# Output projection of a hybrid decoder layer: the order written by hand, operands summed on TensorE, filling steps dealt anew

## The chip, the cores and the metric

The kernel runs on one core of one Trainium2 chip, in one launch. The metric is the device time of the program in microseconds (us), the median of several runs.

## The reference, cut to what matters

One decoder layer on a sequence of 1024 rows of 1024 float32 features: two groups of attention heads, one output projection for both, two normalised residual additions, a feed-forward part of width 2816 and a gated embedding.

```python
xn = rmsnorm(h, pre_mix_norm)
proj = xn @ w_in
ret_out = silu(rg) * head_groupnorm(retention(rope(rq), rope(rk), rv))   # 4 heads of 128
mla_out = mla_causal(q, k, v)                                            # 8 heads, values of 64
mix = concatenate([ret_out, mla_out]) @ w_o
h = h + rmsnorm(mix, post_mix_norm)
hn = rmsnorm(h, pre_ffn_norm)
ff = (silu(hn @ w_gate) * (hn @ w_up)) @ w_down
h = h + rmsnorm(ff, post_ffn_norm)
h = h + rmsnorm(p @ w_ple_proj, ple_norm) * sigmoid(h @ w_ple_gate + b_ple_gate)
```

## The kernel before

Rows are worked in 8 tiles of 128. A float32 product is made of three matmuls on TensorE (PE): each operand is split into a rounded high part and the rest (`split`, L79: a cast on ScalarE, ACT, and a subtraction on VectorE, DVE, or on GpSimd, POOL), and `products` (L89) adds high by high, high by rest and rest by high in a PSUM bank.

**Attention and filling (L576 to L655).** Eight heads run one after the other, each in two halves (`gg`) of two groups (`g`). The first half of the output projection, retention's 512 features by `w_o`, does not depend on these heads. It is the filling: a generator (`product_to`, L546) of 16 steps of 12 matmuls each, two for a row tile, whose results go to memory (`od`). `advance(gen, tag, n)` (L557) lets n steps run. Heads 2 to 5 take 2 steps after their first half and 1 after their second, heads 6 and 7 take 1 after the first, and L655 runs the 2 that are left after the last head.

**Output projection (L705 to L765).** For each of 8 tiles, in the order 0, 2, 4, 6, 1, 3, 5, 7, `project` splits the tile's attention features (`mt` into `mh`, `ml`), multiplies them by the second half of `w_o` (24 matmuls into a double PSUM bank `po3`; there are two such banks), adds the filling's result in `mix` (L715, DVE), takes the root of the mean square (ACT's Square at L717 writes its squares into the PSUM bank; L111 on DVE, L113 on POOL), scales (L719), adds the residual rows in `ht` (L720), stores them to `hd`, takes a second root (Square at L723, again into the bank) and scales again (L725 on DVE, L726 on ACT). `operands` (L728) turns the normalised rows into the operands of the feed-forward part, which multiplies in 7 block products instead of 8, so that it needs sums of blocks: for the first four tiles two transposed halves (B11, B21), for the last four four differences t1 to t4 on POOL (L739 to L742) and five transposed blocks T2, T1, T3, B22, T4. A block is four 128x128 transposes on PE (`to_operand`, L681, into `ptx`), a cast on ACT and a subtraction on DVE. The banks for `ptx` go round in the order t, f, t, o, where t has two.

**Feed-forward part (from L889).** `load(m)` fetches a quarter of a weight matrix, `weight_part` splits it, `weight_sums` makes four sums on POOL, `product(m, n)` is 12 matmuls (`gu`), `evict` empties a bank.

**What sets the order.** Each engine runs its queue in order. A scheduler with times of its own deals the instructions to the queues, so that code order is only a wish, until the `manual_schedule` at L948: under it the order of the code is kept. DMAs all go through SyncE's (SP's) queue.

Of the kernel before, what the change touches and what calls it, by code (L numbers as in the profile page):

```python
# [11 lines left out]
F32 = mybir.dt.float32  # L12
F32R = mybir.dt.float32r
# [49 lines left out]
def hybrid_layer(ctx: ExitStack, tc: tile.TileContext, a: dict, out: bass.AP):  # L63
# [57 lines left out]
    pad.tile([P, 8], F32, name="pad")  # L121
    pack = const.tile([P, sum(PACK.values())], F32, name="pack")
    mhalf = const.tile([P, 32], F32, name="mhalf")
    pool.memset(mhalf, -0.5)

    views, off = {}, 0
# [446 lines left out]
    pm = scoped(st2, "pm", 2)  # L573
    vb = None

    for h in range(NH):  # L576
        kh_, kl_, qh, ql = heads(h) if h else first
        if h == 2:
# [13 lines left out]
        for gg in range(2):  # L592
            cs = slice(gg * 512, (gg + 1) * 512)
            po = ps1("po", "of"[gg] if h >= 3 else "o")
            for g in (2 * gg, 2 * gg + 1):
                pb = []
                sc = ps2("sc") if g < 2 else None
                for i in (2 * g, 2 * g + 1):
                    n = (i + 1) * P
                    c1 = slice(i * P, (i + 1) * P)  # L600
                    if g >= 2:
                        sc = ps2("sc")
                    o = (i % 2) * 512 if g < 2 else 0
                    nc_ = 1 if n <= 512 else 2
                    w = max(n // nc_, 256)
                    for c in range(nc_):
                        products(sc[:, o + c * 512 : o + c * 512 + w],
                                 [(qh[:, c1], ql[:, c1], kh_[:, c * w : (c + 1) * w], kl_[:, c * w : (c + 1) * w])])
                    w = n // nc_
                    sv = sc[:, o : o + nc_ * 512].rearrange("p (c n) -> p c n", c=nc_)[:, :, :w]  # L610
                    nm = small.tile([P, 1], F32, name="nm")
                    dve.tensor_tensor_reduce(  # L612
                        out=sv, in0=sv, in1=cmask[:, S - n :].rearrange("p (c n) -> p c n", c=nc_),
                        scale=-1.0, scalar=3.0e38, op0=ALU.add, op1=ALU.min, accum_out=nm)
                    pr_ = pm.tile([P, S], F32, name="pr", bufs=5)
                    rs = small.tile([P, 1], F32, name="rs")
                    act.activation(pr_[:, :n].rearrange("p (c n) -> p c n", c=nc_), sv, AF.Exp, bias=nm, scale=-1.0,  # L617
                                   accum_out=rs)
                    ri = small.tile([P, 1], F32, name="ri")
                    dve.reciprocal(out=ri, in_=rs)  # L620
                    pool.tensor_tensor(out=pr_[:, :n], in0=pr_[:, :n], in1=ri.broadcast_to([P, n]), op=ALU.mult)  # L621
                    pb.append(pr_)
                last = 2 * g + 1
                for jj in range(g + 1):
                    blk = [(2 * jj, 0), (2 * jj, 1), (2 * jj + 1, 0), (2 * jj + 1, 1)]
                    if jj == g:
                        blk = [blk[0], blk[1], blk[3]]
                    pt = ps1("ptp")
                    for m, (kk, qq) in enumerate(blk):
                        pe.transpose(pt[:, m * P : (m + 1) * P], pb[qq][:, kk * P : (kk + 1) * P], ident)  # L630
                    nn = len(blk) * P
                    th = pm.tile([P, 512], F32R, name="th", bufs=4)[:, :nn]
                    tl = pm.tile([P, 512], F32R, name="tl", bufs=4)[:, :nn]
                    split(th, tl, pt[:, :nn])
                    off = (g % 2) * 256
                    for kk in (2 * jj, 2 * jj + 1):
                        if kk < last:
                            src, dst = slice((kk % 2) * 256, (kk % 2) * 256 + 256), slice(off, off + 256)
                        else:
                            src, dst = slice(256, 384), slice(off + 128, off + 256)  # L640
                        pe.matmul(po[:, dst], vt[:, kk, :], th[:, src], start=(kk == 0), stop=False)  # L641
                        pe.matmul(po[:, dst], vt[:, kk, :], tl[:, src], start=False, stop=(kk == last))  # L642
            if h >= 2:
                advance(gen, "fo"[gg], (2, 1)[gg] if h < 6 else 1 - gg)
            os_ = pm.tile([P, 512], F32, name="os")
            rows = slice((h % 2) * 64, (h % 2) * 64 + 64)
            act.copy(out=os_[rows], in_=po[64:])
            dve.tensor_tensor(out=os_[rows], in0=po[:64], in1=os_[rows], op=ALU.add)
            for i in range(4):
                sp.dma_start(out=mo[4 * gg + i][rows, h // 2, :], in_=os_[rows, i * P : (i + 1) * P])  # L650
        if h == 4:
            wo2 = [slot(a["w_o"][4 + k], name=f"o{4 + k}", hl=(bh[1][:, k, :], bl[1][:, k, :])) for k in range(4)]

    act.activation(small.tile([P, 1], F32, name="warm", bufs=1), rs, AF.Silu)
    advance(gen, "f", 2 * NT)  # L655
    st2.close()
    st3.close()
# [23 lines left out]
    def to_operand(i, j, src, tags="tfto"):  # L681
# [1 line left out]
        pt = ps1("ptx", tags[nblk % len(tags)])  # L683
        nblk += 1
        for k in range(4):
            pe.transpose(pt[:, k * P : (k + 1) * P], src[:, k * P : (k + 1) * P], ident)
        js = slice(j * P, (j + 1) * P)
        split(xs[i][0][:, :, js], xs[i][1][:, :, js], pt.rearrange("p (k n) -> p k n", k=4))

# [12 lines left out]
        sp.dma_start(out=blk[n % 7], in_=od[t])  # L702
        sp.dma_start(out=blk[7 + n % 3], in_=a["x"][t * P : (t + 1) * P])

    def project(n):  # L705
        t = order[n]
        mt = mts[n]
        mh, ml = [pmo.tile([P, 4, P], F32R, name=n_) for n_ in ("mh", "ml")]
        mix, ht = blk[n % 7], blk[7 + n % 3]
        split(mh, ml, mt, sub=pool)  # L710
        pt = ps2("po3")
        for c in range(2):
            cs = slice(c * 512, (c + 1) * 512)
            products(pt[:, cs], [(mh[:, k, :], ml[:, k, :], wo2[k][0][:, cs], wo2[k][1][:, cs]) for k in range(4)])
        dve.tensor_tensor(out=mix, in0=pt, in1=mix, op=ALU.add)  # L715
        ss = small.tile([P, 1], F32, name="s3")
        act.activation(pt, mix, AF.Square, accum_out=ss)  # L717
        rsqrt(ss, ss, 1.0 / D)
        dve.scalar_tensor_tensor(out=mix, in0=mix, scalar=ss, in1=wpm, op0=ALU.mult, op1=ALU.mult)  # L719
        dve.tensor_tensor(out=ht, in0=ht, in1=mix, op=ALU.add)  # L720
        sp.dma_start(out=hd[t], in_=ht)
        ss = small.tile([P, 1], F32, name="s3")
        act.activation(pt, ht, AF.Square, accum_out=ss)  # L723
        rsqrt(ss, ss, 1.0 / D)
        dve.tensor_tensor(out=mix, in0=ht, in1=wpf, op=ALU.mult)  # L725
        act.activation(mix, mix, AF.Copy, scale=ss)  # L726

    def operands(n, part=None):  # L728
        j = n % 4
        mix = blk[n % 7]  # L730
        if n < 4:
            to_operand(B11, j, mix[:, lo_])
            to_operand(B21, j, mix[:, hi_])
        else:
            e, ht = blk[j], blk[7 + n % 3]
            t1, t2, t3, t4 = e[:, lo_], ht[:, lo_], mix[:, lo_], e[:, hi_]
            b11, b12, b21, b22 = e[:, lo_], mix[:, lo_], e[:, hi_], mix[:, hi_]
            if part != 1:
                pool.tensor_tensor(out=t1, in0=b12, in1=b11, op=ALU.subtract)  # L739
                pool.tensor_tensor(out=t2, in0=b22, in1=t1, op=ALU.subtract)  # L740
                pool.tensor_tensor(out=t3, in0=b22, in1=b12, op=ALU.subtract)
                pool.tensor_tensor(out=t4, in0=b21, in1=t2, op=ALU.subtract)  # L742
            for i, src in ((T2, t2), (T1, t1), (T3, t3), (B22, b22), (T4, t4))[slice(*((0, 5), (2, 5), (0, 2))[part or 0])]:
                to_operand(i, j, src)

    load_rows(0)
    load_rows(1)
    load_tiles(0)
    for v, name in ((wpm, "w_post"), (wpf, "w_pref")):
        sp.dma_start(out=v, in_=a[name].broadcast_to([P, D]))  # L750
    for n in range(1, 4):
        if n > 1:
            load_rows(n)
        if n < 3:
            load_tiles(n)
    for n in range(NT):
        if n == 7:
            load_tiles(7)
        project(n)
        if n % 4 < 2:  # L760
            load_rows(n + (4 if n < 4 else 2))
        if n >= 2:
            operands(n - 2)
        if n < 4:
            load_tiles(n + 3)  # L765
    st_m.close()
    st_b.close()

# [118 lines left out]
        todo[i].append((f, args))  # L887

    load(0)  # L889
    load(1)  # L890
    weight_part(0, 0)
    weight_part(1, 0)
    operands(NT - 2)
    for m, n in steps[:2]:
        product(m, n)
    operands(NT - 1, 2)
    for m, n in steps[2:4]:
        product(m, n)
    for m in range(2):
        weight_sums(m)  # L900
    for m, n in steps[:4]:
        evict(m, n)


    for q in range(NQ):
# [42 lines left out]
    with tc.manual_schedule():  # L948
        for i, (m, n) in enumerate(steps):
            if i < 4:  # L950
                continue
            for f, args in todo[i]:
                f(*args)
            if i == 6:
                operands(NT - 1, 1)
            product(m, n)
            evict(m, n)
    st_g.close()
# [209 lines left out]
```

## Time and profile before

| what | value |
| --- | --- |
| median of 3 runs | 1400.54 us (1399.19 to 1403.55) |
| the profiled execution: its own time | 1400.68 us |
| the profiled execution: span from first to last instruction | 1398.9 us |
| granted TensorE clock, mean over the span | 0.986 |
| PE busy | 1336.5 us, 96% of the span |
| DVE, ACT, POOL busy | 770.9, 541.8, 461.8 us |

The profiled execution's time is 0.14 us over the median, and lies 1.8 us over its span. A matmul's end is modelled in the profile, so that PE's busy time is a little more than PE's work: what a matmul takes of a dense row of them is the distance between two starts. The granted clock is 1.0 where the engine has its full 2.4 GHz and 0.5 where it has 1.2 GHz.

### The profile page before, as it was taken

To read this page: it belongs to the slowest core of one execution; us is meant where nothing else is said; L and a number is where in the kernel's file an instruction comes from. 1 tells how busy PE (TensorE), PEld (TensorE's weight loads), DVE (VectorE), ACT (ScalarE), POOL (GpSimd) and SP (SyncE) were. 2 spreads that over 40 slices of the span, in tenths; PEclk is the share of its full clock that TensorE was granted. 3 is DMA by queue.
4 is the path that set the end of the run, shared out by engine and by line. 5 is a ranking of instruction groups with operands and counts; after the bars stand their busy time and mean duration, and the time that the engine had idled before them with its cause. 6 is when DMAs were issued, how large, how long until landed. Compare 5 with 4: busy or idle time off the path is not lost.

```text
span 1398.9 us, 18091 instructions
## 1 busy us (share of the span) xinstructions
PE 1336.5 (96%) x6756; PEld 1134.4 (81%) x6756; DVE 770.9 (55%) x1193; ACT 541.8 (39%) x898; POOL 461.8 (33%) x341
## 2 busy tenths in 40 slices
PE   7999999999989999887999999999999999999997
PEld 6987988988778887665788888888888788888886
DVE  6445637445566676488445444444445554474645
ACT  5443321011565555355343333333334444344521
POOL 1100000000363333248577666666664100012500
PEclk9999999999999999998999999999999999999999
DMA  7127831212474641743344344433346876565422
GB/s 251 46 92 250 265 118 39 75 23 60 143 232 123 200 131 30 273 135 123 121 165 149 146 173 173 169 138 144 140 178 218 269 234 211 178 218 193 138 102 75
DMA packets 85304, 214.73 MB, mean 153 GB/s; under 512 B 8992, under 2 KB 23840, under 8 KB 79584
## 3 DMA queue, kind: packets, MB, share of 16 engines
q1 hardware_dynamic: 85216, 213.58, 45.5%
q8 instruction: 53, 0.87, 0.3%
q14 instruction: 35, 0.29, 0.1%
HBM read 144.86 MB, written 67.63 MB: 152 GB/s over the span
## 4 chain that ended last, share of the span: by engine, by line
PE 83%; DMA 4%; DVE 4%; POOL 3%; issue 3%; ACT 2%; SPq 1%; DVEq 0%; ACTq 0%; POOLq 0%
PE gu L834 29%; PE db L1011 7%; PE pqk L94 6%; PE pg L94 6%; PE da L1011 6%; PE pa L94 4%; PE fill L94 3%; PE prv L94 3%; PE sc L94 3%; PE ptp L630 2%; PE prg L94 2%; PE pge L94 2%; PE po L642 1%; PE pq L94 1%; PE po L641 1%
## 5 line engine op out<-in xcount | busy, mean ns | idle before, releaser
L834 PE MATMUL gu<-x,gh 128*128 128x512 f32 x1232 | 383.6, 393 | 6.3 <-ACT po L723 5.6
L834 PEld LDWEIGHTS gu<-x,gh 128*128 128x128 f32 x1232 | 233.2, 190 | 55.7 <-ACT po L723 5.8
L834 PE MATMUL gu<-x,gl 128*128 128x512 f32 x616 | 241.2, 392 | 0.4 <-DVE gl L82 0.4
L834 PEld LDWEIGHTS gu<-x,gl 128*128 128x128 f32 x616 | 116.7, 189 | 25.1 <-DVE gl L82 0.7
L845 ACT COPY duo<-gu 128x512 f32<-128x512 f32 x66 | 38.9, 589 | 189.3 <-PE gu L834 189.3
L621 POOL TENSOR_TENSOR pr<-pr,ri 128x128 f32<-128x128 f32 (+3 forms) x64 | 74.8, 1178 | 105.7 <-DVE ri L620 98.4
L113 POOL TENSOR_TENSOR s<-s,mhalf 128x1 f32<-128x1 f32 x32 | 23.9, 752 | 238.4 <-DVE s L111 238.3
L113 POOL TENSOR_TENSOR gf<-gf,mhalf 128x4 f32<-128x4 f32 x8 | 8.1, 1008 | 266.7 <-DVE gf L111 266.7
L82 DVE TENSOR_TENSOR gl<-strip,gh 128x1024 fp32r<-128x1024 f32 (+1 forms) x44 | 61.6, 1399 | 33.3 <-ACT gh L81 33.3
L82 DVE TENSOR_TENSOR x<-draw,x 128x1024 fp32r<-128x1024 f32 (+1 forms) x43 | 48.1, 1135 | 46.9 <-ACT x L81 46.9
L82 DVE TENSOR_TENSOR gl<-graw,gh 128x1024 fp32r<-128x1024 f32 x22 | 33.8, 1538 | 72.5 <-ACT gh L81 72.5
L81 ACT CAST x<-draw 128x1024 fp32r<-128x1024 f32 (+1 forms) x47 | 45.2, 979 | 73.0 <-PE db L1011 20.6
L82 DVE TENSOR_TENSOR gl<-duo,gh 128x1024 fp32r<-128x1024 f32 x22 | 29.5, 1343 | 67.9 <-ACT gh L81 67.9
L850 DVE TENSOR_TENSOR duo<-gu,duo 128x512 f32<-128x512 f32 x66 | 45.4, 687 | 38.0 <-PE gu L834 37.9
L82 DVE TENSOR_TENSOR tl<-ptp,th 128x512 fp32r<-128x512 f32 (+1 forms) x80 | 49.8, 633 | 24.7 <-ACT th L81 23.7
L94 PE MATMUL pg<-x,x 128*128 128x512 f32 (+1 forms) x255 | 58.9, 378 | 0.0
L81 ACT CAST th<-ptp 128x512 fp32r<-128x512 f32 (+1 forms) x80 | 42.4, 544 | 41.9 <-PE ptp L630 41.6
L855 POOL TENSOR_TENSOR duo<-duo 128x512 f32<-128x512 f32 x11 | 23.3, 2122 | 103.2 <-DVE duo L818 103.2
L617 ACT ACTIVATE pr<-sc,nm 128x128 f32<-128x128 f32 (+3 forms) x64 | 47.7, 747 | 18.7 <-DVE nm L612 11.1
L94 PEld LDWEIGHTS pg<-x,x 128*128 128x128 f32 x255 | 45.8, 188 | 8.6
L612 DVE CUSTOM_DVE_ANT_0 sc<-sc,cmask 128x128 f32<-128x128 f32 (+3 forms) x64 | 48.0, 770 | 7.7 <-PE sc L94 7.3
L94 PE MATMUL pqk<-bl,hi_r 128*128 128x512 f32 x128 | 50.7, 396 | 0.0
(368 smaller groups left out, 3418.5 us busy)
## 6 DMA issues: line engine op xcount, KB each, us to landing
draw<-ld SPq DMA_DIRECT2D x58, 256.0 KB, 3.8
graw<-in_w_gate SPq DMA_DIRECT2D x11, 1024.0 KB, 8.6
duo<-in_w_up SPq DMA_DIRECT2D x11, 1024.0 KB, 4.7
duo<-in_w_down SPq DMA_DIRECT2D x11, 1024.0 KB, 5.1
td<-duo SPq DMA_DIRECT2D x11, 1024.0 KB, 4.4
ld<-duo SPq DMA_DIRECT2D x11, 1024.0 KB, 4.4
draw<-td SPq DMA_DIRECT2D x36, 256.0 KB, 4.1
ld<-duo SPq DMA_DIRECT2D x11, 768.0 KB, 6.7
```

The source lines that it names most:

```text
L81: act.copy(out=hi, in_=src)
L82: sub.tensor_tensor(out=lo, in0=src, in1=hi.bitcast(F32), op=ALU.subtract)
L94: pe.matmul(dst, l, r, start=(m == 0), stop=(m == n - 1))
L113: pool.tensor_tensor(out=dst, in0=dst, in1=mhalf[:, :n], op=ALU.pow)
L612: dve.tensor_tensor_reduce(out=sv, in0=sv, in1=cmask[:, S - n :].rearrange("p (c n) -> p c n", c=nc_), scale=-1.0, scalar=3.0e38, op0=ALU. ...
L617: act.activation(pr_[:, :n].rearrange("p (c n) -> p c n", c=nc_), sv, AF.Exp, bias=nm, scale=-1.0, accum_out=rs)
L621: pool.tensor_tensor(out=pr_[:, :n], in0=pr_[:, :n], in1=ri.broadcast_to([P, n]), op=ALU.mult)
L630: pe.transpose(pt[:, m * P : (m + 1) * P], pb[qq][:, kk * P : (kk + 1) * P], ident)
L834: pe.matmul(dst, l[:, at, ks], r[:, k, :], start=(n in (0, 1, 3) and x == 0), stop=(x == 11), skip_group_check=True)
L845: act.copy(out=s[nm], in_=dst)
L850: dve.tensor_tensor(out=s[nm], in0=dst, in1=s[nm], op=ALU.add)
L1011: pe.matmul(banks[j], l[:, ls], r[:, rs_], start=(fresh and q == 0 and m == 0), stop=(q == NQ - 1 and m == 2), skip_group_check=True)
```

## The change

- The order of the output projection and of the start of the feed-forward part is written by hand: `manual_schedule` now encloses L756 ff. and L889 ff. A turn `turn(n)` works three tiles at once: tile n's sum, roots and scaling, tile n - 1's second root and last scaling, tile n - 2's operands, and the matmuls of tile n + 1, whose rows were split a turn earlier.
- Square writes its squares to `junk`, a corner of the operand T4 in SBUF, no longer into the PSUM bank.
- POOL makes two differences a tile (t1, t3) in place of four. T2 = b22 - t1 and T4 = b21 - b22 + t1 are summed in PSUM: each 128x128 block is multiplied by the identity or by its negative (`minus`) as an ordinary float32 matmul, 2 and 3 of them where one transpose stood.
- The 16 filling steps are dealt anew: heads 2 to 7 take 1, 3, 2, 2, 2 and 0; three stand in the last group of head 7, one ahead of each of its first three pairs of products; 3 are left after the last head.

```diff
+    FILL = (0, 1), (2, 1), (1, 1), (1, 1), (1, 1), (0, 0)
...
+                    if h == NH - 1 and g == 3 and jj < 3:
+                        advance(gen, "o", 1)
...
-                advance(gen, "fo"[gg], (2, 1)[gg] if h < 6 else 1 - gg)
+                advance(gen, "fo"[gg], FILL[h - 2][gg])
...
+    dve.tensor_scalar(out=minus, in0=ident, scalar1=-1.0, scalar2=None, op0=ALU.mult)
...
-            pe.transpose(pt[:, k * P : (k + 1) * P], src[:, k * P : (k + 1) * P], ident)
+            ks = slice(k * P, (k + 1) * P)
+            if len(src) == 1:
+                pe.transpose(pt[:, ks], src[0][:, ks], ident)
+                continue
+
+            for n, v in enumerate(src):
+                pe.matmul(pt[:, ks], v[:, ks], (ident, minus)[n % 2], start=(n == 0), stop=(n == len(src) - 1))
...
+    def squares(n, i, v):
+        ss = roots[n, i] = small.tile([P, 1], F32, name="s3")
+        act.activation(junk, v.rearrange("p (b n) -> p b n", b=8), AF.Square, accum_out=ss)
+
+    def sums(n):
+        e, mix, ht = blk[n % 4], blk[n % 7], blk[7 + n % 3]
+        pool.tensor_tensor(out=ht[:, lo_], in0=mix[:, lo_], in1=e[:, lo_], op=ALU.subtract)
+        pool.tensor_tensor(out=ht[:, hi_], in0=mix[:, hi_], in1=mix[:, lo_], op=ALU.subtract)
...
+        return [(T2, j, (b22, t1)), (T1, j, (t1,)), (T3, j, (t3,)), (B22, j, (b22,)), (T4, j, (b21, b22, t1))]
...
+    def turn(n):
+        mix, ht = blk[n % 7], blk[7 + n % 3]
+        own, last = n < NT, 1 <= n
+        ops = operand_list(n - 2) if n >= 2 else []
+        if own:
+            dve.tensor_tensor(out=mix, in0=banks_o[n], in1=mix, op=ALU.add)
+        if last:
+            rsqrt(roots[n - 1, 1], roots[n - 1, 1], 1.0 / D)
+        for o in ops[:2]:
+            to_operand(*o)
+        if own:
+            squares(n, 0, mix)
+        if last:
+            act.activation(blk[(n - 1) % 7], blk[(n - 1) % 7], AF.Copy, scale=roots[n - 1, 1])
+        if own:
+            rsqrt(roots[n, 0], roots[n, 0], 1.0 / D)
+        if n - 1 >= 4:
+            sums(n - 1)
+        for o in ops[2:]:
+            to_operand(*o)
+        if own:
+            if n + 2 < NT:
+                prepare(n + 2)
+            if n + 1 < NT:
+                out_product(n + 1)
+            dve.scalar_tensor_tensor(out=mix, in0=mix, scalar=roots[n, 0], in1=wpm, op0=ALU.mult, op1=ALU.mult)
+            dve.tensor_tensor(out=ht, in0=ht, in1=mix, op=ALU.add)
+            sp.dma_start(out=hd[order[n]], in_=ht)
+            squares(n, 1, ht)
+            dve.tensor_tensor(out=mix, in0=ht, in1=wpf, op=ALU.mult)
...
+    with tc.manual_schedule():
+        turn(NT - 1)
+        load(1)
+        weight_part(0, 0)
+        for m, n in steps[:2]:
+            product(m, n)
+        turn(NT)
+        weight_part(1, 0)
+        for m, n in steps[2:4]:
+            product(m, n)
+        for o in operand_list(NT - 1)[:2]:
+            to_operand(*o)
+        for m in range(2):
+            weight_sums(m)
+        for m, n in steps[:4]:
+            evict(m, n)
...
+            if i == 6:
+                for o in operand_list(NT - 1)[2:]:
+                    to_operand(*o)
```

What stands in DVE's queue in the middle of the output projection, before (`duo` holds `mix` and `ht`; L715 adds the projection, L719 scales, L720 adds the residual, L725 multiplies by the next norm's weights, L111 belongs to a root, L82 is an operand's rest):

```order
L111 TENSOR_SCALAR s_5940<-s_5940 128x1
L719 SCALAR_TENSOR_TENSOR duo_5741<-duo_5741,s_5940,strip 128x1024
L720 TENSOR_TENSOR duo_5742<-duo_5742,duo_5741 128x1024
L715 TENSOR_TENSOR duo_5738<-po_5973,duo_5738 128x1024
L725 TENSOR_TENSOR duo_5741<-duo_5742,strip 128x1024
L111 TENSOR_SCALAR s_5947<-s_5947 128x1
L82 TENSOR_TENSOR x_5728<-ptx,x_5728 128x4x128
L82 TENSOR_TENSOR x_5729<-ptx,x_5729 128x4x128
L111 TENSOR_SCALAR s_5999<-s_5999 128x1
```

The same place after the change (L755, L775, L776 and L779 are the former L715, L719, L720 and L725):

```order
L111 TENSOR_SCALAR s_5962<-s_5962 128x1
L775 SCALAR_TENSOR_TENSOR duo_5743<-duo_5743,s_5962,strip 128x1024
L776 TENSOR_TENSOR duo_5744<-duo_5744,duo_5743 128x1024
L779 TENSOR_TENSOR duo_5743<-duo_5744,strip 128x1024
L755 TENSOR_TENSOR duo_5740<-po_5971,duo_5740 128x1024
L111 TENSOR_SCALAR s_5999<-s_5999 128x1
L82 TENSOR_TENSOR x_5730<-ptx,x_5730 128x4x128
L82 TENSOR_TENSOR x_5731<-ptx,x_5731 128x4x128
L111 TENSOR_SCALAR s_6022<-s_6022 128x1
```

The multiplication by the weights moved from behind the next tile's sum to ahead of it.

What stands in ACT's queue where the feed-forward part begins, before (L717 and L723 are the two Squares of the last tile, `gh` the high half of the first weights, `x` those of the operands):

```order
L726 ACTIVATE duo_5740<-duo_5740,s_6122 128x1024
L81 CAST x_5734<-ptx 128x4x128
L81 CAST gh_6262<-graw 128x1024
L81 CAST x_5733<-ptx 128x4x128
L81 CAST x_5731<-ptx 128x4x128
L717 ACTIVATE po_6173,s_6199<-duo_5741 128x1024
L81 CAST x_5730<-ptx 128x4x128
L81 CAST gh_6256<-duo_5738 128x1024
L81 CAST x_5732<-ptx 128x4x128
L845 COPY duo_5739<-gu 128x512
L723 ACTIVATE po_6173,s_6206<-duo_5742 128x1024
```

The same place after the change (L733 is Square, L763 the last scaling):

```order
L733 ACTIVATE x_5736,s_6250<-duo_5743 128x8x128
L763 ACTIVATE duo_5742<-duo_5742,s_6206 128x1024
L81 CAST x_5734<-ptx 128x4x128
L81 CAST x_5735<-ptx 128x4x128
L81 CAST x_5736<-ptx 128x4x128
L733 ACTIVATE x_5736,s_6289<-duo_5744 128x8x128
L81 CAST gh_6223<-graw 128x1024
L81 CAST x_5732<-ptx 128x4x128
L81 CAST x_5733<-ptx 128x4x128
L763 ACTIVATE duo_5743<-duo_5743,s_6289 128x1024
```

The first weights' cast moved from ahead of both Squares of the last tile to behind both.

## Rows read from the trace of the kernel before

**Rows 1.** Stretches of core 0: us, busy time (instructions) of each engine, granted clock, DMA.
```profile
550.00:572.00 22.00, 17.95 (x71) 14.15 (x72) 6.19 (x11) 7.52 (x14) 2.92 (x2) 0.77 0.21 57
572.00:681.00 109.00, 85.63 (x379) 67.73 (x378) 76.81 (x82) 51.93 (x82) 63.56 (x51) 0.89 0.47 170
...
650.00:660.00 10.00, 4.42 (x20) 3.49 (x19) 8.70 (x8) 4.36 (x8) 8.77 (x6) 0.79 0.13 52
```

**Rows 2.** Timeline of PE: start, us, line, operation; two matmuls of a projection.
```profile
574.17 0.39 PE L94 MATMUL po<-bh,ml 128*128 128x512 f32 x1
574.40 0.39 PE L94 MATMUL po<-bh,mh 128*128 128x512 f32 x1
```

**Rows 3.** PE in the retention: float32 matmuls (`psc`), transposes (`pkt`), the next start.
```profile
308.02 1.05 PE L462 MATMUL psc<-qk 128*128 128x128 f32 x8
308.91 0.60 PE L469 MATMUL pkt<-pack,qk 128*128 128x128 f32 x4
309.27 0.48 PE L94 MATMUL pqk<-bh,hi_r 128*128 128x512 f32 x1
```

**Rows 4.** Instructions of the tile `psc`: count, ns min/median/max.
```profile
L462 PE MATMUL psc<-qk x64: 270/275/275, 197.1 to 348.1; 128*128 128x128 f32 x64
```

**Rows 5.** Chain that ended last: twelve operand transposes at full clock.
```profile
679.55 1.31 PE ptx L686 x12
```

**Rows 6.** What PE waited for from 540 to 720: us in total, times, longest.
```profile
PE po L94 <- ACT po L723: 9.2, 6, 3.6
PE gu L834 <- ACT po L723: 5.6, 1, 5.6
PE ptx L686 <- POOL duo L740: 2.6, 3, 1.2
PE ptx L686 <- DVE x L82: 2.1, 1, 2.1
PE ptx L686 <- POOL duo L739: 1.8, 1, 1.8
...
PE ptx L686 <- POOL duo L741: 1.1, 1, 1.1
```

**Rows 7.** Single lines from 560 to 690: count, ns min/median/max, first and last start.
```profile
L715 DVE TENSOR_TENSOR duo<-po,duo x8: 1210/1218/1225, 578.1 to 646.3; 128x1024 f32<-128x1024 f32 x8
L717 ACT ACTIVATE po<-duo x8: 1029/1034/1047, 579.3 to 647.6; 128x1024 f32<-128x1024 f32 x8
L717 ACT ACTIVATION_READ_ACCUMULATOR po<-duo x8: 186/193/202, 580.3 to 648.5; 128x1 f32 x8
L719 DVE SCALAR_TENSOR_TENSOR duo<-duo,s,strip x8: 1283/1284/2344, 581.3 to 651.3; 128x1024 f32<-128x1024 f32 x8
L720 DVE TENSOR_TENSOR duo<-duo,duo x7: 1224/2168/2277, 582.6 to 654.7; 128x1024 f32<-128x1024 f32 x7
L725 DVE TENSOR_TENSOR duo<-duo,strip x8: 1207/1430/1728, 584.9 to 657.5; 128x1024 f32<-128x1024 f32 x8
L111 DVE TENSOR_SCALAR s<-s x16: 136/141/154, 580.5 to 659.7; 128x1 f32<-128x1 f32 x16
L113 POOL TENSOR_TENSOR s<-s,mhalf x16: 541/550/560, 580.7 to 663.7; 128x1 f32<-128x1 f32 x16
```

**Rows 8.** Operand and weight splits: tiles `ptx` and `gh`.
```profile
L81 ACT CAST x<-ptx x28: 565/586/611, 594.7 to 682.0; 128x512 fp32r<-128x512 f32 x28
L82 DVE TENSOR_TENSOR x<-ptx,x x28: 673/676/692, 595.3 to 683.9; 128x512 fp32r<-128x512 f32 x28
L81 ACT CAST gh<-graw x2: 1052/1054/1056, 643.0 to 677.3; 128x1024 fp32r<-128x1024 f32 x2
```

**Rows 9.** POOL's differences of two tiles (L740) from 560 to 690.
```profile
L740 POOL TENSOR_TENSOR duo<-duo,duo x2: 2128/2129/2130, 624.4 to 634.6; 128x512 f32<-128x512 f32 x2
L740 POOL TENSOR_TENSOR duo<-duo x2: 1281/1438/1596, 644.0 to 667.8; 128x512 f32<-128x512 f32 x2
```

**Rows 10.** The DMAs of L702 that fetch a tile of `od`.
```profile
DMA to landing us min/median/max: 5.1/8.3/11.0
```

More of the change, by code (lines that the diff above doesn't have):

```diff
@@ L123, in hybrid_layer @@
     mhalf = const.tile([P, 32], F32, name="mhalf")
+    minus = const.tile([P, P], F32, name="minus")
     pool.memset(mhalf, -0.5)
@@ L703, in load_tiles, with prepare, out_product @@
         sp.dma_start(out=blk[7 + n % 3], in_=a["x"][t * P : (t + 1) * P])
[L705 to L711, printed above, removed]
+    junk = xt[6][:, :, :, 3 * P :].rearrange("p h k n -> p (h k) n")
+    split_rows, banks_o, roots = {}, {}, {}
+    def prepare(n):
+        split_rows[n] = [pmo.tile([P, 4, P], F32R, name=n_) for n_ in ("mh", "ml")]
+        split(*split_rows[n], mts[n], sub=pool)
+    def out_product(n):
+        mh, ml = split_rows[n]
+        pt = banks_o[n] = ps2("po3")
         for c in range(2):
@@ L714, in project, with operand_list @@
             products(pt[:, cs], [(mh[:, k, :], ml[:, k, :], wo2[k][0][:, cs], wo2[k][1][:, cs]) for k in range(4)])
[L715 to L728, printed above, removed]
+    def squares(n, i, v):
[5 more added lines that the diff above has]
+        pool.tensor_tensor(out=ht[:, hi_], in0=mix[:, hi_], in1=mix[:, lo_], op=ALU.subtract)
+    def operand_list(n):
         j = n % 4
@@ L731, in operands @@
         if n < 4:
[L732 to L744, printed above, removed]
+            return [(B11, j, [mix[:, lo_]]), (B21, j, [mix[:, hi_]])]
+        e, ht = blk[j], blk[7 + n % 3]
+        b21, b22, t1, t3 = e[:, hi_], mix[:, hi_], ht[:, lo_], ht[:, hi_]
+        return [(T2, j, (b22, t1)), (T1, j, (t1,)), (T3, j, (t3,)), (B22, j, (b22,)), (T4, j, (b21, b22, t1))]
[29 more added lines that the diff above has]
+            dve.tensor_tensor(out=mix, in0=ht, in1=wpf, op=ALU.mult)
     load_rows(0)
@@ L750, in hybrid_layer @@
         sp.dma_start(out=v, in_=a[name].broadcast_to([P, D]))
[L751 to L765, printed above, removed]
+    load_rows(2)
+    load_tiles(1)
+    load_rows(3)
+    load_tiles(2)
+    with tc.manual_schedule():
+        prepare(0)
+        load_rows(4)
+        prepare(1)
+        load_rows(5)
+        out_product(0)
+        for n in range(NT - 1):
+            turn(n)
+            if n < 4:
+                load_tiles(n + 3)
+            if n in (2, 3):
+                load_rows(n + 4)
+            if n == 6:
+                load_tiles(7)
     st_m.close()
@@ L889, in hybrid_layer @@
     load(0)
[L890 to L902, printed above, removed]
+    with tc.manual_schedule():
+        turn(NT - 1)
[13 more added lines that the diff above has]
+            evict(m, n)
     for q in range(NQ):
```

2 lines of the change are left out of this document (removed).

## The prediction

> **What bounds the kernel now.** I read the page's busy times first: PE is busy for 96% of the span, so that most stages are limited by PE's own work and the change can win only where PE waits. The stretches come next [rows 1]. From 550 to 572 (the last head's second half and what is left of the filling) and from 572 to 681 (the output projection, up to the last operand of the feed-forward part) the granted clock is 0.77 and 0.89, where the whole span has 0.986. These are the two places that the change touches. In the second, PE's work at full clock is 192 matmuls of the projection and 72 of the feed-forward part at 0.23 us from start to start [rows 2] and 112 operand transposes at 1.31/12 = 0.109 us [rows 5], that is 60.7 + 12.2 = 72.9 of 109.0 us. So 36 us there are waits, half clock and short gaps. The list of waits names most of them [rows 6]: the next projection and the first weights' product wait for the Square that still holds the PSUM bank (9.2 + 5.6 us), the operands for POOL's differences (2.6 + 1.8 + 1.1) and for a bank that DVE has not emptied (2.1). Together 22.4 us.
>
> **What the change removes.** Square no longer writes to the bank, so the first two waits, 14.8 us, lose their cause. T2 and T4 no longer come from POOL, whose second difference takes 1.28 to 2.13 us [rows 9]. All 22.4 us are taken off, since every queue is dealt anew, and what waits in the new order is counted below.
>
> **PE's added work.** Four tiles each have 8 + 12 ordinary float32 matmuls where 8 transposes stood: 80 matmuls for 32 transposes. The retention has both kinds side by side [rows 3]: eight instructions of `psc` fill 308.91 - 308.02 = 0.89 us, four transposes 0.36. The code asks for 32 products in `psc` and the trace has 64 [rows 4], so one product is two instructions, 0.222 us; a transpose is one, 0.09 to 0.109. The work grows by 80 x 0.222 - 32 x 0.109 = 17.8 - 3.5 = **14.3 us**. It is certain as work, and it lies on the path unless it falls into a pause; its place is between the last projections and the first weights' products, where PE is what everything waits for. The Trainium skill (TensorE: Matmul & The Clock Gate, Terms) says that transpose mode is 4x faster for FP32. By that an estimate would be 80 x 0.436 - 3.5 = 31.4 us of added work; the rows show a factor of 2, and they decide.
>
> **A turn in the middle.** The order rows of DVE show the new loop. Tile n's Square needs its sum (L715); the sum now stands behind the weights' multiplication (L725) of the tile before, and that one behind the residual sum (L720), which needs the scaling (L719), which needs the root. Per turn [rows 7]: Square 1.03 + 0.19, L111 0.14, L113 0.55, L719 1.28, L720 1.22 alone or 2.17 beside POOL's split, L725 1.43, L715 1.22, which is 7.1 to 8.0, with 0.2 for the hand-offs 7.3 to 8.2 us. PE has 24 x 0.228 + 8 x 0.109 = 6.3 us of work in such a turn. So PE pauses 1.0 to 1.9 us in each of five turns; I take 1.4, together **7.0 us** (5.0 to 9.5). Before, the sum stood ahead of the multiplication, and the same loop was shorter by 1.43.
>
> **The first tile with five operands.** T4 goes into the bank that T2 had, and T2's rest (L82, on DVE) stands behind a sum and a multiplication. **2.0 us**, the nearest row being the 2.1 us that PE waits for such a bank now [rows 6]; 0 to 4.
>
> **The start of the feed-forward part.** The order rows of ACT show that the first weights' cast now stands behind both Squares of the last tile. In DVE's queue, from that tile's sum on: sum 1.22, root 0.14, T2's rest 0.68; then PE's twelve matmuls of T4, 2.66; T4's cast and rest, 0.59 + 0.68 [rows 8]; scaling 1.28, residual sum 1.22 to 2.17, Square 1.22, the weights' cast 1.05: 10.7 to 11.7, taken as 11.2 us. PE has 20 x 0.222 + 12 x 0.109 = 5.7 us of operands meanwhile. The sum itself waits for the last tile of `od`: its fetch stands in SP's queue behind the store of the tile before, which waits for that tile's residual sum, and such a fetch lands 5.1 us after its issue at the least [rows 10]. The residual sum and the last projection's matmuls (5.5 us) run at about the same time; I take 4 us from the end of these matmuls to the landing, 0 to 8. So PE pauses 4 + 11.2 - 5.7 = **9.5 us** (5 to 14).
>
> **Behind it.** The second weights' cast stands behind five casts of operands: the cast 1.05 and its rest, less what runs beside, **2.5 us** (1 to 4). The last tile's T2 is cast behind the casts of weight sums, which wait for POOL; six of POOL's operations of 1.3 to 2.1 us [rows 9] run against 7.7 us of PE's work, **4.0 us** (0 to 8). New pauses in all: 7.0 + 2.0 + 9.5 + 2.5 + 4.0 = 25.0 us, 11 to 39.5.
>
> **The filling.** From 550 to 572 PE is busy for 17.95 of 22 us, and a granted clock of 0.77 means 10.1 us at 1.2 GHz, which cost 5.1 [rows 1]: at most 9.1 us to win. Three steps of 12 x 0.228 = 2.7 us now stand in the last group, where they cover the softmax's round through DVE, ACT and POOL and should keep the clock up. They are not new work; four steps fewer stand in heads 2 to 6 and open pauses there, 0 to 2.7 us each. I take the clock's 5.1 less 1.8, **3.3 us** won (0 to 9.1).
>
> **The clock from 572 to 681.** 0.89 of 109 us means 24 us at 1.2 GHz, at most 12.0 us lost [rows 1]. The pauses that brought it down go, others as long come: no term, -12 to +6 in the range.
>
> **The sum.** 14.3 - 22.4 + 25.0 - 3.3 = +13.6 us. Against the profiled execution's own 1400.68 us, which is 0.14 over the median, this is 1414 us, 1% slower.
>
> **The rivals.**
> 1. PE is fed. The place is the loop of a turn: if the sum finds DVE free and the loop falls to PE's 6.3 us, the turns lose nothing; with that, the last tile's sums run earlier against PE, so that the 9.5 us become 3. It decides where the new pauses are 11 us or less, as the lower bounds say. With 3 us of half clock saved: 14.3 - 22.4 + 11 - 3.3 - 3 = -3.4, 1397; with the filling's whole 9.1, 1391. For it speaks that the bank is freed 6 us earlier, against it that DVE's loop is longer by L725 in the rows themselves. Taken at 1393, faster.
> 2. A draw: the new pauses are 15 instead of 25 us, and a little clock is won: 1402.
> 3. The clock stays up. From 650 to 660, with PE busy for 4.42 us and POOL for 8.77, the granted clock is 0.79 [rows 1]. If more matmuls and shorter pauses keep it at full from 572 to 681, up to 12.0 us come back: 1414 - 9 = 1405, still slower. The Trainium skill (TensorE: Matmul & The Clock Gate, Part 4: PE-mode transpose) says that transposes do not count as busy for the gate the way matmuls do, which speaks for this rival; in the rows nothing separates the two, and the pauses of the start, 9.5 us, remain.
> 4. The plain float32 matmul with the identity costs four transposes: 14.3 becomes 31.4, 1431. The 64 instructions of `psc` speak against it.
>
> **How the numbers follow.** Chances: forecast (1407 to 1422) 0.72, PE fed 0.10, draw 0.07, clock up 0.09, four transposes 0.02. The likeliest gives **1414 us**. About 0.3%, 4.2 us, is what a measurement of this kernel can tell from no change. Faster by more, under 1396.3: 0.10. Within: the draw's 0.07. Slower, over 1404.7: the rest, 0.83. The range leaves out the fed case and the four transposes, and part of the draw: 1401 to 1422.
>
> **What would show it.** In the changed kernel's profile: `ptx` has 80 more PE instructions on the line of `matmul` in `to_operand` than products, 160 in all, at 0.11 us each from start to start; the Square is gone from the list of PE's waits; turns four to six are 7.3 to 8.2 us apart; the longest pause of PE is ahead of the first `gu` and its releaser is ACT's cast of `gh`; the clock from 550 to 565 is full. The prediction is wrong if turns are 6.5 us apart, if that pause is under 4 us, or if the last operand comes less than 112 us behind the first projection.

## The result, and the profile after

The changed kernel takes 1412.01 us (median of four runs, 1409.36 to 1413.17), the kernel before 1400.4 on the same chip: ratio 1.0085, 95% interval 1.0065 to 1.0106, slower by 11.6 us. Forecast were 1414 us and a range of 1401 to 1422. The profiled execution took 1410.94 us, its span is 1409.1.

The stretches of the kernel after stand beside [rows 1] (us, busy time and instructions of PE, PEld, DVE, ACT and POOL, granted clock, DMA share, GB/s):

```profile
550.00:572.00 22.00, 18.26 (x90) 14.31 (x89) 5.52 (x9) 3.47 (x6) 2.56 (x2) 1.00 0.41 148
572.00:695.00 123.00, 101.45 (x522) 83.74 (x521) 75.65 (x87) 54.00 (x87) 43.79 (x38) 0.93 0.40 142
...
650.00:660.00 10.00, 6.93 (x22) 5.14 (x23) 3.31 (x4) 2.08 (x3) 0.55 (x1) 0.66 0.45 157
```

The end of the last head runs at full clock in this execution, and the first projection starts 4.5 us earlier, at 567.4 instead of 571.9, with one step of the filling, 2.7 us, now behind its first twelve matmuls (571.2 to 573.9). The last operand of the feed-forward part comes at 690.4 instead of 680.6. So the stage between them takes 123.0 us instead of 108.7, with that step in it, and all that was lost was lost there. PE's waits in it (us in total, times, longest), beside [rows 6]:

```profile
PE gu L872 <- ACT gh L81: 7.6, 2, 6.0
PE po L94 <- POOL ml L82: 3.5, 5, 0.7
PE ptx L698 <- DVE x L82: 3.2, 2, 2.6
PE ptx L694 <- ACT duo L763: 2.5, 4, 0.8
PE gu L872 <- DVE duo L888: 2.4, 1, 2.4
PE ptx L698 <- POOL duo L737: 1.8, 1, 1.8
```

No wait for a Square is left, and the list from 565 to 700 still adds up to 22.6 us, where the kernel before has 24.3 (the 22.4 of [rows 6], and three more rows of 0.8 and less). The change has exchanged one set of waits for another, nearly as long, and PE has 14.3 us more to do. The chain that ended last shows the order in which the new ones come (start, us, what):

```profile
633.80 1.24 DVE duo L776
635.06 0.32 SPq L777
635.48 4.92 DMA duo<-od
640.49 1.23 DVE duo L755
...
642.43 4.58 PE ptx L698 x24
...
649.57 1.24 DVE duo L776
650.89 1.15 ACT x L733 x2
652.04 0.94 ACT gh L81
653.01 1.23 DVE gl L82
654.31 6.48 PE gu L872 x22
...
663.68 1.05 ACT duo L763
664.80 1.27 POOL duo L737
...
667.30 1.24 POOL strip L831
...
677.11 1.05 ACT gh L81
...
680.70 0.61 DVE duo L888
681.36 5.74 PE gu L872 x24
```

The last sum (L755) waits for a fetch of `od` that SP issues behind a store; the first weights' cast stands behind the last tile's second Square (L733); and POOL comes to the sums of the weights (L831) only behind the last tile's differences (L737).

### The profile page after: what moved, and what is told of

Its sections match the earlier page's. It is cut to its first block, busy times and chain, and to the rows that moved or that the text cites. A ratio compares the mean times of both kernels' runs of the same rounds, so it can differ in the third digit from the quotient of the medians.

```text
span 1409.1 us, 18348 instructions
## 1 busy us (share of the span) xinstructions
PE 1348.0 (96%) x6884; PEld 1146.9 (81%) x6884; DVE 769.4 (55%) x1194; ACT 541.6 (38%) x898; POOL 444.0 (32%) x333
## 4 chain that ended last, share of the span: by engine, by line
PE 82%; DVE 5%; issue 4%; DMA 3%; ACT 3%; POOL 2%; SPq 0%; ACTq 0%; DVEq 0%; POOLq 0%
PE gu L872 29%; PE db L1053 8%; PE pqk L94 6%; PE pg L94 6%; PE da L1053 6%; PE pa L94 4%; PE prv L94 3%; PE sc L94 3%; PE fill L94 3%; PE prg L94 2%; PE pge L94 2%; PE ptp L633 1%; PE pq L94 1%; PE po L647 1%; DVE duo L776 1%
## 5 line engine op out<-in xcount | busy, mean ns | idle before, releaser
L883 ACT COPY duo<-gu 128x512 f32<-128x512 f32 x66 | 38.9, 589 | 184.9 <-PE gu L872 184.9
L82 DVE TENSOR_TENSOR gl<-strip,gh 128x1024 fp32r<-128x1024 f32 (+1 forms) x44 | 61.0, 1386 | 39.0 <-ACT gh L81 39.0
L82 DVE TENSOR_TENSOR x<-draw,x 128x1024 fp32r<-128x1024 f32 (+1 forms) x43 | 48.3, 1136 | 45.1 <-ACT x L81 44.8
L82 DVE TENSOR_TENSOR gl<-graw,gh 128x1024 fp32r<-128x1024 f32 x22 | 31.8, 1447 | 68.5 <-ACT gh L81 68.5
L888 DVE TENSOR_TENSOR duo<-gu,duo 128x512 f32<-128x512 f32 x66 | 45.4, 688 | 38.5 <-PE gu L872 37.3
L82 DVE TENSOR_TENSOR gl<-duo,gh 128x1024 fp32r<-128x1024 f32 x22 | 29.5, 1342 | 67.5 <-ACT gh L81 67.5
L82 DVE TENSOR_TENSOR tl<-ptp,th 128x512 fp32r<-128x512 f32 (+1 forms) x80 | 49.6, 633 | 17.4 <-ACT th L81 16.0
```

Source lines behind the costliest of these rows:

```text
L82: sub.tensor_tensor(out=lo, in0=src, in1=hi.bitcast(F32), op=ALU.subtract)
L883: act.copy(out=s[nm], in_=dst)
L888: dve.tensor_tensor(out=s[nm], in0=dst, in1=s[nm], op=ALU.add)
```

## Experiments

All were run beside the kernel before on their own chips (median 1396 to 1397 there); what counts is the ratio. 0.001 is 1.4 us.

**The filling.** `fill_alone` is the kernel before with the new filling, `old_filling` the changed kernel with the old one.

```diff
...
-                advance(gen, "fo"[gg], (2, 1)[gg] if h < 6 else 1 - gg)
+                advance(gen, "fo"[gg], FILL[h - 2][gg])
```

> The kernel before with the new dealing of the 16 filling steps and nothing else; the output projection keeps the scheduler's order. The prediction's step on the filling (3.3 us won, 0 to 9.1) gives 1397 us, with the clock full from 550 to 565 and the first projection matmul 2 to 5 us earlier than at 571.9. Rival: the four steps missing in heads 2 to 6 open as much as the last head wins, 1400 to 1401.

> The changed kernel with the old dealing of the filling: the hand order and the sums on TensorE alone. If the filling is worth the same under either order, 1412 + 3.3 = 1415 us. Rival: the hand order hides what the filling won, 1412.

Alone: 0.9993 (0.9976 to 1.0009), 1.0 us won, with an interval of 3.4 won to 1.3 lost, so that the 3.3 us of the forecast lie at its edge. The change with the old filling: 1.0085 (1.0065 to 1.0104), the same as with the new. The stretch from 550 to 572 in `fill_alone`, and then in two kernels with the old filling, `old_filling` and `sums_alone`:

```profile
550.00:572.00 22.00, 19.52 (x91) 15.71 (x90) 5.39 (x8) 3.47 (x6) 2.58 (x2) 0.92 0.45 159
...
550.00:572.00 22.00, 15.95 (x85) 11.70 (x84) 8.06 (x14) 8.57 (x15) 3.52 (x3) 1.00 0.27 84
...
550.00:572.00 22.00, 17.94 (x86) 13.31 (x87) 5.07 (x8) 4.88 (x10) 3.40 (x3) 1.00 0.41 137
```

The ten profiled kernels with the new filling have a clock of 0.92 to 1.00 there. But the four with the old one, whose matmuls stand in the same order in the last head's second half and up to the projection, have 0.77 (before), 0.61 (`square_off_the_bank`), 1.00 and 1.00. So the half clock that the kernel before shows there belongs to the profiled execution, and is not shown to belong to the old filling. The first projection of `fill_alone` starts 5.0 us earlier (566.9), with one filling step, 2.7 us, still behind it, and the order of the projection then is another. What the filling wins by itself can't be told from nothing, and behind the fixed order it can't be seen.

**PE's sums without the fixed order.** `sums_alone` is the kernel before with T2 and T4 summed in PSUM and nothing else of the change; the scheduler deals.

```diff
...
-                pool.tensor_tensor(out=t2, in0=b22, in1=t1, op=ALU.subtract)
...
-                pool.tensor_tensor(out=t4, in0=b21, in1=t2, op=ALU.subtract)
-            for i, src in ((T2, t2), (T1, t1), (T3, t3), (B22, b22), (T4, t4))[slice(*((0, 5), (2, 5), (0, 2))[part or 0])]:
+            for i, src in ((T2, (b22, t1)), (T1, t1), (T3, t3), (B22, b22), (T4, (b21, b22, t1)))[slice(*((0, 5), (2, 5), (0, 2))[part or 0])]:
```

> The kernel before with T2 and T4 summed in PSUM by 80 float32 matmuls where 32 transposes stood, POOL making two differences instead of four; order by the scheduler, old filling. Theory A (the prediction's: the added 14.3 us of TensorE work lie on the path): 1400.4 + 14.3 less the 5.5 us of waits for POOL = 1409 us. Theory B (a dealt order puts the added work into pauses that POOL's differences made, and it is the fixed order that costs): 1399 to 1402.

Here the last tile's T3 and T4 read a buffer after a fetch of `w_down` has overwritten it; number and size of the instructions are those of the change, and `filling_and_sums` below, which reads it before the fetch and has the new filling too, is as fast within the noise. Ratio 0.9989 (0.9975 to 1.0004). The 14.3 us of work are there (the same 160 instructions), but PE's waits from 565 to 700 have shrunk from 24.3 to 11.9 us, by about as much, and the granted clock there is 0.96 instead of 0.90:

```profile
PE po L94 <- ACT po L731: 8.0, 6, 3.6
PE gu L840 <- ACT gh L81: 2.5, 1, 2.5
...
```

So added work on PE, busy for 96% of the span, cost nothing that can be measured where it fell into waits that were there anyway.

**The fixed order, all of it and by halves.** The changed kernel without either block of fixed order; with that of the turns 0 to 6 alone; and with that of the last two turns and the first products alone. Each edit replaces one or both of two lines:

```diff
-    with tc.manual_schedule():
+    if True:
```

> The changed kernel with its code in the same order but without the two fixed-order blocks, so that the scheduler deals the turns again. Theory A (the added work and the lost bank waits decide): 1408 to 1412 us, close to the changed kernel. Theory B (the fixed order itself costs 10 us or more): 1398 to 1403.

> The changed kernel with the fixed order for the turns of the output projection (turns 0 to 6) and the scheduler's order for the last two turns and the start of the feed-forward part. Theory B1 (the cost of the fixed order lies at the start of the feed-forward part, where the first weights' cast stands behind both Squares of the last tile: the 9.5, 2.5 and 4.0 us of the prediction): 1394 to 1398 us on a chip where the kernel before takes 1397 to 1400. Theory B2 (it lies in the turns, whose loop of 8.0 us is over TensorE's 6.3): no gain, 1405 to 1410.

> The complement: turns 0 to 6 dealt by the scheduler, the last two turns and the start of the feed-forward part in the fixed order. Theory B1: 1410 to 1418 us, as slow as the change or slower. Theory B2: 1398 to 1402.

Without: 1.0019 (1.0002 to 1.0036). Projection only: 0.9990 (0.9969 to 1.0012). Start only: 1.0124 (1.0097 to 1.0150). The whole loss lies in the second block, the fixed order in which the feed-forward part begins. The first block has the turns 8 us apart as the change has, and loses nothing. PE's waits with the first block alone, 13.4 us in all from 565 to 700:

```profile
PE po L94 <- POOL ml L82: 2.9, 4, 0.7
PE ptx L698 <- POOL duo L737: 2.7, 2, 1.8
PE ptx L694 <- ACT duo L763: 2.5, 4, 0.8
PE ptx L698 <- ACT duo L763: 2.3, 2, 1.8
PE ptx L698 <- DVE x L82: 1.8, 1, 1.8
```

The waits for `gh` and for L888 are gone, 10.0 us, and the last operand comes 108.1 us behind the first projection. In the same kernel ACT casts the first weights ahead of the last tile's second Square, and POOL sums the weights from 647 on, ahead of the last tile's differences (timeline: start, us, engine, line, operation, tiles, idle time before):

```profile
645.55 1.05 ACT L81 CAST gh<-graw 128x1024 fp32r<-128x1024 f32 x1
647.43 2.21 POOL L831 TENSOR_TENSOR strip<-graw 128x512 f32<-128x512 f32 x1 [1.94 <-DVE duo L775]
650.81 1.06 ACT L733 ACTIVATE x<-duo 128x1024 fp32r<-128x1024 f32 x1 [0.57 <-DVE duo L776]
663.77 1.27 POOL L737 TENSOR_TENSOR duo<-duo 128x512 f32<-128x512 f32 x1 [0.94 <-ACT duo L763]
```

In the changed kernel POOL stands idle instead, with the weights' sums queued behind what it waits for:

```profile
664.80 1.27 POOL L737 TENSOR_TENSOR duo<-duo 128x512 f32<-128x512 f32 x1 [9.81 <-ACT duo L763]
...
667.25 1.28 POOL L831 TENSOR_TENSOR strip<-graw 128x512 f32<-128x512 f32 x1
```

**PE's sums within the fixed order.** `fixed_order_pool_sums` is the change with POOL's four differences and plain transposes.

```diff
-        pool.tensor_tensor(out=ht[:, lo_], in0=mix[:, lo_], in1=e[:, lo_], op=ALU.subtract)
-        pool.tensor_tensor(out=ht[:, hi_], in0=mix[:, hi_], in1=mix[:, lo_], op=ALU.subtract)
+        pool.tensor_tensor(out=e[:, lo_], in0=mix[:, lo_], in1=e[:, lo_], op=ALU.subtract)
+        pool.tensor_tensor(out=ht[:, lo_], in0=mix[:, hi_], in1=e[:, lo_], op=ALU.subtract)
+        pool.tensor_tensor(out=mix[:, lo_], in0=mix[:, hi_], in1=mix[:, lo_], op=ALU.subtract)
+        pool.tensor_tensor(out=e[:, hi_], in0=e[:, hi_], in1=ht[:, lo_], op=ALU.subtract)
```

> The changed kernel with POOL's four differences a tile and plain transposes again, everything else as in the change: 14.3 us less of TensorE work under the fixed order. Theory A (the added work lies on the path): 1407 to 1412 less 14.3, plus the 3 to 5.5 us of waits for POOL, 1397 to 1402. Theory B (the chain over DVE and ACT decides, the added work fills its pauses): 2 to 4 us less than the change.

Ratio 1.0083 (1.0052 to 1.0113), no gain: theory A fails, and the 2 to 4 us of theory B can't be told from none. PE has 14.3 us less to do and waits 33.4 us instead of 22.6:

```profile
PE gu L874 <- ACT gh L81: 11.1, 2, 8.6
PE ptx L694 <- POOL s L113: 8.0, 1, 8.0
PE ptx L694 <- POOL duo L738: 5.0, 1, 5.0
...
```

It is an exchange, not a subtraction: the waits grew by 10.8 us, partly for POOL's two further differences. That some of the work had lain in these pauses is the likely reason, argued from the sums and not shown by itself.

**The order of the start.** `scaling_first` puts scaling, residual sum and store of every turn ahead of the last three operands; `start_with_early_cast` does so for the last tile alone, and puts the first weights' cast ahead of the second Square and the first two products ahead of the late operands.

```diff
+        if n == NT - 1:
+            dve.scalar_tensor_tensor(out=mix, in0=mix, scalar=roots[n, 0], in1=wpm, op0=ALU.mult, op1=ALU.mult)
+            dve.tensor_tensor(out=ht, in0=ht, in1=mix, op=ALU.add)
+            sp.dma_start(out=hd[order[n]], in_=ht)
+            weight_part(0, 0)
+            squares(n, 1, ht)
+            dve.tensor_tensor(out=mix, in0=ht, in1=wpf, op=ALU.mult)
+            for m, k in steps[:2]:
+                product(m, k)
         for o in ops[2:]:
             to_operand(*o)
...
```

> The changed kernel with one step moved in each turn: the scaling, the residual sum and the store stand ahead of the last three operands' rests instead of behind them. By the prediction's chain at the start of the feed-forward part this takes T4's matmuls, cast and rest (2.7 + 0.6 + 0.7 us) and two further rests out of the way to the first weights' cast, so that its 6 us pause falls to 2 or 3 and the time by 3 to 4 us. Rival (what is behind that pause then ends last: second weights, last tile's T2): within 1 us of the change.

> The changed kernel, with the last tile's turn in another fixed order: scaling, residual sum and store first, then the cast of the first weights ahead of the second Square, and the first two weights' products ahead of the late operands of tile 5. Theory A (the longest pause costs what it shows): the wait of the first weights' product for the cast, 6.0 us, and part of that behind it go, and the time is 1403 to 1407. Theory B (any fixed order of this stretch moves the same 30 us of pauses to another place, since DVE, ACT and POOL end last together): the pause ahead of the first product is under 2 us, others stand ahead of the operands, and the time is 1409 to 1415.

Ratios 1.0088 (1.0062 to 1.0114) and 1.0100 (1.0071 to 1.0128): neither helps. In `scaling_first` the longest pause, ahead of the first weights' product, falls only from 6.0 to 4.2 us, and the wait for L889, the former L888, grows from 2.4 to 4.0: its rival was right. Theory B of the second gave the right time, but not for its reason alone: the pause ahead of the first product, which should have fallen under 2 us, is as long as before, and others have grown:

```profile
PE gu L881 <- ACT gh L81: 7.7, 2, 6.1
PE gu L881 <- DVE duo L897: 4.0, 1, 4.0
PE gu L881 <- DVE gl L82: 3.7, 2, 3.2
```

The cast comes at 645.13 instead of 651.95, and its product at 646.23, nearly 7 us earlier. But PE has nothing left to do meanwhile, since the operands that stood in that pause now stand behind the product. Within what is left of the pause, 6.1 us, the last sum waits 4.0 us for its fetch, and behind the sum the first Square and a scaling stand ahead of the cast in ACT's queue. In the chain of this run the store of the tile before is issued at 636.28, the fetch behind it, and the last sum starts at 641.49, when the fetch has landed.

```profile
636.28 0.32 SPq L786
...
636.70 4.70 DMA duo<-od
```

POOL's sums of the weights start at 668.20 there, at 664.28 in `scaling_first`, at 671.27 in `fixed_start_only`, and at 647.43 in the one kernel of fixed turns that loses nothing. In the kernel before they start at 649.46, in `sums_alone` at 645.15, in `filling_and_sums` at 643.69.

**The loop of a turn.** `multiplication_behind_sum` moves the multiplication by the weights (L779) behind the next tile's sum.

```diff
...
+            dve.tensor_tensor(out=blk[(n - 1) % 7], in0=blk[7 + (n - 1) % 3], in1=wpf, op=ALU.mult)
...
-            dve.tensor_tensor(out=mix, in0=ht, in1=wpf, op=ALU.mult)
```

> The changed kernel with one instruction moved: the multiplication by the weights (L779) of tile n-1 stands behind the sum of tile n (L755), no longer ahead of it. Loop theory (the prediction's): the 8 us between two turns are DVE's and ACT's loop, which gets 1.4 us shorter, so turns are 6.5 to 6.9 us apart, five pauses go, and the time is 1405 (1403 to 1408). Rival: the turns are 8 us apart for what stands behind the loop too (operands of the tile two before, which now come later, and the last tile's multiplication behind the first weights' rest), and the loop is not worth anything by itself: 1411 to 1420, with the longest pause of PE still ahead of the first weights' product or ahead of the last tile's operands.

It takes 1435.78 us, 1.0272 (1.0242 to 1.0302), and tells little on the loop. The input rows of the tile three later go into the same buffer, and their fetch now stands ahead of the multiplication in the program; so for the first four tiles it reads those rows, and it waits for them:

```profile
DVE duo L757 <- DMA duo<-in_x: 17.5, 3, 6.7
```

In the one early turn without that wait the sums are 6.7 us apart (580.81, 587.55), as the loop theory said, and 8.0 in the change; in a late turn without it they are 7.8 apart (641.63, 649.44), and 9.0 in the change. So the loop does get shorter. What that is worth in time is not settled by this run; `fixed_projection_only`, whose turns are 8 to 9 us apart at no loss, speaks for little or nothing.

**The bank.** `square_off_the_bank` is the kernel before with both Squares writing to the corner of T4 that the change uses, where nothing reads them.

```diff
...
-        act.activation(pt, mix, AF.Square, accum_out=ss)
+        act.activation(junk_s, mix.rearrange("p (b n) -> p b n", b=8), AF.Square, accum_out=ss)
...
```

> The kernel before with one part of the change: both Squares of the projection write to a buffer in SBUF that nothing reads, so that they no longer hold the PSUM bank. The prediction's term: the waits of 9.2 and 5.6 us lose their cause, so up to 14.8 us go, 1382 to 1390. Rival: the bank was only the last of several things that came at about the same time (the tile's own sum, the root, the operands of POOL); another releaser is named in the list of PE's waits with most of the same time, and the kernel takes 1394 to 1398, no measurable change against some 1397.

Ratio 1.0010 (0.9989 to 1.0032). The waits for Square are gone, and most of the same time stands ahead of the operands, now for POOL:

```profile
PE ptx L686 <- POOL duo L741: 11.7, 3, 7.5
PE gu L836 <- DVE gl L82: 3.3, 1, 3.3
PE ptx L686 <- ACT duo L728: 2.8, 1, 2.8
```

Its granted clock from 565 to 700 is 0.86, where the kernel before has 0.90, which may hide part of what the freed bank won: from the first projection to the last operand this execution takes 106.6 us instead of 108.7.

**Two parts together.** `filling_and_sums` has the new filling and PE's sums, dealt by the scheduler; in it the last tile's rows are read ahead of the fetch of `w_down`.

> The kernel before with two parts of the change and no order by hand: the new filling, and T2 and T4 summed in PSUM by float32 matmuls. The scheduler deals the rest. Each alone gave a ratio of 0.999. If they add up and the scheduler hides PE's 14.3 us of added work again: 1393 to 1396, faster by a hair than before. Rival: the two change the order that the scheduler finds, and the work is no longer hidden: 1400 to 1410.

Ratio 0.9995 (0.9977 to 1.0014), waits of 12.1 us: as fast as before, neither faster by a hair nor as slow as the rival. No version here beats the kernel before by more than can be measured.

**What adds up.** PE's added work and the change of PE's listed waits from 565 to 700, against the measured difference (ratio less one, times 1398):

| kernel | added work | waits | work + change of waits | measured, us |
|---|---|---|---|---|
| before | 0 | 24.3 | 0 | 0 |
| the change | 14.3 | 22.6 | +12.6 | +11.9 (9.1 to 14.8) |
| fixed_start_only | 14.3 | 25.6 | +15.6 | +17.3 (13.6 to 21.0) |
| start_with_early_cast | 14.3 | 25.6 | +15.6 | +14.0 (9.9 to 17.9) |
| scaling_first | 14.3 | 23.4 | +13.4 | +12.3 (8.7 to 15.9) |
| fixed_order_pool_sums | 0 | 33.4 | +9.1 | +11.6 (7.3 to 15.8) |
| fixed_projection_only | 14.3 | 13.4 | +3.4 | -1.4 (-4.3 to +1.7) |
| sums_alone | 14.3 | 11.9 | +1.9 | -1.5 (-3.5 to +0.6) |
| square_off_the_bank | 0 | 22.9 | -1.4 | +1.4 (-1.5 to +4.5) |
| fill_alone | 0 | 19.5 | -4.8 | -1.0 (-3.4 to +1.3) |
| old_filling | 14.3 | 22.5 | +12.5 | +11.9 (9.1 to 14.5) |
| filling_and_sums | 14.3 | 12.1 | +2.1 | -0.7 (-3.2 to +2.0) |
| change_without_fixed_order | 14.3 | 16.3 | +6.3 | +2.7 (0.3 to 5.0) |
| multiplication_behind_sum (565 to 730) | 14.3 | 38.9 | +28.9 | +38.0 (33.8 to 42.2) |

The sums agree with the times to some 5 us in all but the last, which loses 9 us more than they say. They separate the kernels that lose some 12 us or more from those that lose little or nothing; the execution of `change_without_fixed_order` that was profiled took 1406.5 us, 6.7 over its median, so that its 6.3 is too much. Of the rest the clock explains part: `fixed_projection_only` has a granted clock of 0.98 from 565 to 700, the kernel before 0.90.

## Why the prediction was right

**Added work, 14.3 us.** The count and the price hold: 96 + 64 instructions on the matmul line of `to_operand`, 2.68 us for 24 of them at full clock, 0.112 each. The 4x of the Trainium skill (TensorE: Matmul & The Clock Gate, Terms) is a factor of 2 here, since a product is two instructions and a transpose one. The step that is right only under a condition is "it lies on the path unless it falls into a pause". Where the scheduler deals, nearly all of it falls into pauses (`sums_alone`); and in the fixed order taking it out wins nothing (`fixed_order_pool_sums`). That its 14.3 us came out right in the sum is most likely because the pauses were counted for that order, with this work standing in some of them.

**Removed waits, 22.4 us.** The waits for Square went, as the list shows; one of 1.8 us for POOL's differences is left (L737). That nearly all of the time comes back if the bank alone is freed (`square_off_the_bank`) bears out counting the new waits separately, and shows that freeing the bank alone was no way to gain the 14.8 us.

**Turns, 7.0 us.** The sums of turns four to six are 8.0 to 9.0 us apart (600.96, 609.30, 617.35, 626.36), forecast 7.3 to 8.2: two of the three lie above. In the turns PE waits for POOL's splits and ACT's scalings, 2.9 + 2.5 = 5.4 us, within the range; the rest of the rows on `ml` and `mh`, 1.2, stands ahead of the first turn. The size was about right; that they cost as much in time is not shown, since the same 5.4 us stand in `fixed_projection_only`.

**T4's bank, 2.0 us.** In the first tile with five operands it is 0.6. The second has 2.6, but there T2's rest stands behind the late sum of the last tile: this is part of the start.

**The start, 9.5 us.** From the end of the last projection's matmuls (636.55) to the first weights' product (653.03) are 16.5 us, less 5.7 of operands 10.8. The releaser is the cast of `gh`, behind the last Square, behind a fetch that lands 3.9 us after these matmuls (640.4, forecast 4). Of the 10.8 us the list has 2.6 and 6.0; 1.9 are half clock, 4.58 instead of 2.68 us for 24 operand matmuls.

**Behind it, 2.5 and 4.0 us.** Measured 1.6 for the second cast, and 2.4 for an addition on DVE (L888) that empties a bank and stands behind the rests of the last tile's T2 and T1; the chain to it through POOL's weight sums is the one forecast. New pauses in all: 25.0 forecast, 22.6 listed.

**The filling, 3.3 us.** Mis-sized. Alone it wins 1.0 us with an interval that holds zero, and in the change nothing that can be measured. The step that failed is taking the clock's loss of one profiled execution for the old filling's: two of the four kernels with the old filling run that stretch at full clock. Whether an earlier end of the last head would be spent again in the stage behind it, which waits on DVE, ACT and POOL, these runs leave open. A slip beside it: heads 2 to 6 have 10 steps instead of 13, three fewer and not four.

**The clock, no term.** From 565 to 700 it went from 0.90 to 0.94, not to full, and the rival on it fell: it dropped behind the new pauses. As to the rule that transposes do not count as busy the way matmuls do (the Trainium skill, TensorE: Matmul & The Clock Gate, Part 4): the fixed order has 0.94 with matmuls and 0.89 with transposes, as it would have it, but with 10.8 us more of pauses in the second, so these runs do not separate the two.

**The sum.** That it came within 2 us owes something to luck: the new pauses were 2.4 us shorter than forecast, and the filling's 3.3 us were not won, two errors that nearly cancel. The two largest terms beside them, 22.4 off and 25.0 on, were right as a pair: an order dealt anew moves the pauses.

**What stays open.** Which of the three late things of the start decides: the fetch of `od` behind the store, the first weights' cast, or POOL's weight sums behind the last tile's differences. Moving the cast alone did not help. A fixed order with the fetch ahead of the store, or with POOL's sums of the weights ahead of L737, was not tried. That POOL's order matters is argued from the starts of its weight sums in the runs (643.7 to 649.5 in the kernels above that lose nothing, 664.3 to 671.3 in the change and five more with the fixed start), and not shown by itself.

## What to carry to other kernels

Take an order by hand apart by its stretches: here the turns could be fixed at no cost, and the seam to the next stage, where the queues of five engines must mix two kinds of work, lost some 13 us against the scheduler's order. When a wait is removed, ask what else comes at about the same time, because PE's next releaser was only just behind the bank; and when work is added to the busiest engine, compare it with that engine's listed waits before counting it. In a fixed order look for an engine that is idle while work for the next stage stands queued behind the instruction it waits in, as POOL did for 9.8 us.

## What was not expected of the hardware

The pauses of the start cost more than their length. In the changed kernel the granted clock is at half speed from 643.2 to 646.6, behind PE's wait of 2.6 us, and from 650.0 to 656.9, in and behind its wait of 6.0 us, and full again in the busy stretch after:

```profile
640.00:650.00 10.00, 4.57 (x24) 4.38 (x24) 6.23 (x10) 3.73 (x6) 3.60 (x4) 0.83 0.31 128
...
660.00:670.00 10.00, 7.76 (x59) 6.78 (x58) 4.49 (x6) 4.62 (x7) 5.12 (x4) 1.00 0.01 2
```

From 642 to 647 the 24 operand matmuls lost 1.9 us; the first 24 products, in a stretch at 0.66 (650 to 660), took 7.6 instead of 5.5 us and lost another 2.1. The other stretches at half clock of this kernel (622.7 to 626.1, 670.5 to 673.9) and those of `fixed_projection_only` (to 566.1, and 665.1 to 668.5) cost some 3 and 2 us. So half clock explains 4 to 5 us of the difference between the two, and with the 9.2 us by which the waits are longer (22.6 and 13.4) that is some 14 us, against 13.3 by the two ratios. With the fixed turns alone, where PE was busy for 9.91 of the 10 us from 638 to 648, the clock was full.
